# Seven products for the first head groups of pairs 2 and 3, and a new order around them

## The chip, the core and the metric

The kernel runs on one core of one Trainium2 chip. TensorE (PE, with its weight loads PEld) multiplies, VectorE (DVE) and ScalarE (ACT) work on tiles, GpSimd (POOL) and SyncE (SP) mostly issue transfers. The metric is device time in microseconds of one launch; shorter is better.

## What is computed

Two layers on a sequence of 512 tokens of width 1024, each with a SwiGLU feed-forward (width 2816) behind it, and a last RMS norm. The first layer's mixer is attention over three groups of eight heads of width 128: each group has its own query, key and value columns and its own window and dilation, and a softmax over the groups' log-sums joins them. The second layer's mixer is an mLSTM of eight heads.

```python
def dilated_attention_mixer(xn, positions, w_in, w_out):
    proj = (xn @ w_in).reshape(B, S, N_GROUPS, 3, ATTN_HEADS, ATTN_HEAD_DIM)
    for g, (window, dilation) in enumerate(DIL_CONFIGS):
        q = apply_partial_rope(proj[:, :, g, 0], positions) * scale
        k = apply_partial_rope(proj[:, :, g, 1], positions)
        o, lse = dilated_window_attention(q, k, proj[:, :, g, 2], window, dilation)
        ...
    wts = jax.nn.softmax(jnp.stack(lses), axis=0)
    o = jnp.einsum('gbsh,gbshd->bshd', wts.astype(xn.dtype), jnp.stack(outs))
    return o.reshape(B, S, ATTN_WIDTH) @ w_out

def reference(...):
    for i in range(DEPTH):
        h = h + (attention if i % 2 == 0 else mlstm)(rms_norm(h, ...))
        h = h + swiglu(rms_norm(h, ffn_norm[i]), ffn_w_in[i], ffn_w_out[i])
    return rms_norm(h, final_norm)
```

## The kernel before, in words

Every large matrix is multiplied in float32 as three products of a high and a low part: `split_chunk` (L216) makes a weight chunk's high part by a copy on ACT (L223) and its low part by a difference on DVE (L225), and PE runs high x high, high x low and low x high.

**The work in attention.** The eight heads go in four pairs (`project_pair`, L1003), each with groups 0, 1 and 2. A group's queries and keys for a pair are one 1024 x 512 projection. *Plain* (`project`, L260) it is 96 matmuls of 512 columns in four chunks of weights; its results leave by copies (L1033). *By seven products* (`qk_unit`, L902, a Strassen-like scheme) the weights are four quarters W11, W12, W21, W22; the names P1 to P7 are the products, in the order `QK_ORDER` (L861), each of 24 matmuls of 256 columns. `prepare_part` (L880) makes the weights of one product: up to one difference of quarters (L885), then the split, then the loads of the next group's quarters. `finish` (L913) takes sums out of PSUM by ACT copies and two DVE sums (L937). `by_products` (L865) says which groups go so: groups 1 and 2 of every pair.

**After the projections**, per pair (`attention_pair`, L658): `rope` (L603) turns the first 32 rows of queries and keys, packed four quarters to a tile, by four DVE instructions, and ACT or POOL copies them back (L628). `scores0` (L694) multiplies queries by keys for group 0 and takes masked maxima on DVE (L709); `scores12` (L726) does so for groups 1 and 2 (L734, L737), group by group. `exponentials` (L744) run on ACT. `joint` (L779) exchanges maxima and sums between the groups through one small matmul (`xps`, L770) and makes weights; `weigh(i)` (L797) scales head i's exponentials by them on DVE (L802, L805); `transposes(i)` (L807, L811) and `bring(i)` (L817) turn them through DRAM into `pT`; `values(i)` (L822) multiplies them by the values, 30 small matmuls a head.

**What sets the order.** Each engine takes its instructions in one order that the program writes, with edges added by hand: `tc.issue_after(ins)` puts what is traced inside it behind `ins` on its engine; `behind_scores` and `behind_factors` do so for splits on DVE and ACT. A counter of ticks runs along the projections: `advance` (L143) adds one, four times in a plain or seven-product group, and `defer(n, fn)` (L140) puts work n ticks on. So `SCORES0_AT` (L36) is the tick after group 0 at which its scores come, and `RUN_AT` (L37) has, counted from the start of the next pair, the tick of `scores12`, those of joint, weigh, transposes and bring, those of the two heads' values, and those of the loads of the value tiles. `LAST_AT` is the same for the last pair, whose projections are followed by four chunks of value projection (`a3g12v`) and the output projection (`awo`). A `Feed` (L280) holds weight chunks that are split ahead of their product.

**Later parts.** In the mLSTM, `HEAD_AT` (L40) gives each head three ticks, for `decay` (L2112: one matmul, a mask on DVE, ten exponentials on ACT), `scores` (L2128) and `numerators` (L2139). What is due at one tick runs in the order in which it was deferred (L2196). At the end of the kernel, `ends` (L2367) handles the last two blocks of 128 output rows: add, squares (L2300), root and one Newton step (`newton`, L2353), scale, store.

Of the kernel before, what the change touches and what calls it, by code (L numbers as in the profile page):

```python
# [73 lines left out]
def tile_hybrid_dilated_attn_mlstm(  # L74
# [139 lines left out]
    splits = itertools.count()  # L214

    def split_chunk(chunk):  # L216
# [7 lines left out]
        with behind_scores():  # L224
            nc.vector.tensor_tensor(lo[:, :n], raw[:, :n], hi[:, :n].bitcast(F32), op=ALU.subtract)  # L225
        return view(hi), view(lo)
# [177 lines left out]
    with ExitStack() as actx:  # L404
# [9 lines left out]
        mask_band, mask_causal, mask_dil, perm = part(K_MA, 2 * P), part(K_M1, P), part(K_M2, P), part(K_G, P)  # L414
        cosn = ap.tile([P, SEQ], F32, name="cosn")
# [242 lines left out]
        def attention_pair(pr, qks):  # L658
# [35 lines left out]
            def scores0(q, k):  # L694

                for i in range(2):
                    for b2 in range(2):
# [9 lines left out]
                        for b, o, w in parts:  # L707
                            pb = max(2 * b - 1, 0)
                            nc.vector.tensor_tensor_reduce(  # L709
                                p0[i][:, pb:pb + w // P, :].rearrange("p a b -> p (a b)"),  # L710
                                sp[:, o:o + w], mask_band[:, 2 * P - w:], 1.0, -3e38,
                                op0=ALU.add, op1=ALU.max, accum_out=own[:, 0, 0, i, b:b + 1])
                ahead_of_splits[0] = last_on(DVE)
# [4 lines left out]
                if pr < HEADS // 2 - 1:  # L718
                    exps()
                    ahead_of_splits[0], ahead_of_casts[0] = last_on(DVE), last_on(ACT)  # L720
                else:
                    defer(2, lambda: behind(exps, engine=ACT))
# [3 lines left out]
            def scores12(gs=(1, 2)):  # L726

                for g in gs:
# [6 lines left out]
                for g, i in [e for e in ((1, 0), (2, 0), (1, 1), (2, 1)) if e[0] in gs]:  # L735
# [5 lines left out]
                    if g == 2:  # L741
                        exponentials(1, i)

            def exponentials(o, i):  # L744

                if o:
                    nc.vector.tensor_tensor(own[:, 0, 1, i], mx[:, 0, i], mx[:, 1, i], op=ALU.max)
                nc.vector.tensor_scalar(nb[:, o, i], own[:, 0, o, i], -QK_SCALE, None, op0=ALU.mult)
                if o == 0:
# [47 lines left out]
            def weigh(i):  # L797
                cf4 = weight[0]
                for b in range(4):
                    pb = max(2 * b - 1, 0)  # L800
                    blk = p0[i][:, pb:2 * b + 1, :].rearrange("p a b -> p (a b)")
                    nc.vector.tensor_scalar(blk, blk, cf4[:, 0, i, b:b + 1], None, op0=ALU.mult)  # L802
                for c in range(4):
                    blk = p12[i].rearrange("p (g c) k -> p c g k", g=2)[:, c]
                    nc.vector.tensor_scalar(blk, blk, cf4[:, 1, i, c:c + 1], None, op0=ALU.mult)  # L805
# [59 lines left out]
        def by_products(pr, g):  # L865
            return g > 0

        def load_part(pr, g, key):
            if g > 2:
                return  # L870
# [7 lines left out]
            parts_of.setdefault((pr, g), {})[key] = t  # L878

        def prepare_part(pr, g, name):  # L880
# [10 lines left out]
            elif name == "P7":  # L891
                less("W12", "W22", "W12")
            whl = split_chunk((b[src], 1024, four_k, "a%dg%d%s" % (pr, g, name)))
            if name == "P7":
                less("W21", "W21", "W11")
                for key in ("W11", "W12"):
                    load_part(pr, g + 1, key)
            elif name in ("P3", "P4"):
                load_part(pr, g + 1, src)
            return whl  # L900

        def qk_unit(pr, g, qk):  # L902
# [9 lines left out]

            def finish(name):  # L913
                nonlocal rot, vu
                if name == "P5":
                    vu = ap.tile([P, 2, SEQ], F32, tag="vu", name=nm + "vu")
                    nc.scalar.activation(vu[:, 0], acc["p5"], AF.Copy)
# [4 lines left out]
                elif name in ("P2", "P4"):  # L922
                    th = int(name == "P4")
                    src = two_m(acc[target[name]])
                    if th == 0:
                        t = ap.tile([P, 2, SEQ], F32, tag="rot", name="rot")
                        rot = t[:, 0], t[:, 1]
                    pack(th, src[:R])
                    nc.scalar.activation(halves(qk[0], th), src, AF.Copy)
                    ahead_of_casts[0] = last_on(ACT)  # L930
                    if last and th:
                        rope(qk, rot, False, 1, 2, True)
                elif name in ("P7", "P3"):
                    th = int(name == "P7")
                    out = halves(qk[1], th)
                    with behind_scores():
                        nc.vector.tensor_tensor(out, two_m(acc[target[name]]), two_m(vu[:, 1 - th]), op=ALU.add)  # L937
                    if g == 2:
                        ahead_of_splits[0] = last_on(DVE)
                    pack(2 + th, out[:R])  # L940
                    if g == 2:
                        ahead_of_casts[0] = last_on(ACT)
                    if last and th == 0:
                        rope(qk, rot, False, 0, 1, True)
                        rope(qk, rot, False, 2, 4, True)

            for n, name in enumerate(QK_ORDER):
# [3 lines left out]
                if name == "P5":  # L951
                    acc["u"] = acc_tile(nm + "u")
                    nc.scalar.activation(acc["u"], acc["c11"], AF.Copy)
                    ahead_of_casts[0] = last_on(ACT)
# [32 lines left out]
                if n == 6 and last:  # L987
                    ahead_of_splits[0] = last_on(DVE)
                if n == 6 and not last:
                    back = rope(qk, rot, False)  # L990
                    if g == 2:
                        back()
                        ahead_of_splits[0], ahead_of_casts[0] = last_on(DVE), last_on(ACT)
                    else:
                        defer(1, lambda: behind(back, engine=ACT))
                if n in (1, 3, 5, 6):
                    advance()
                if n:
                    feed.fill(feed.ahead + 1)
            if pr:  # L1000
                feed.ahead = 3

        def project_pair(pr, qks, then=None):  # L1003
            nm = "a%d" % pr
            for g in range(3):
# [5 lines left out]
                if by_products(pr, g):  # L1011
                    qk.extend(tok_tile("%sg%d_%s" % (nm, g, "qk"[part])) for part in range(2))
                    qk_unit(pr, g, qk)
# [915 lines left out]
    with ExitStack() as mctx:  # L1929
# [302 lines left out]
    with ExitStack() as fctx:  # L2232
# [134 lines left out]
        def ends(acc, tb, cs):  # L2367
# [17 lines left out]
            tb2, scaled = held.pop()  # L2385
            r2 = fr[:, tb2:tb2 + 1]
# [3 lines left out]
            rows2 = slice(tb2 * P, (tb2 + 1) * P)  # L2390
# [3 lines left out]
            nc.sync.dma_start(out[rows2, 0:512], scaled)  # L2394
            r = after(DVE_, lambda: newton(tb))
            after(ACT_, lambda: nc.scalar.activation(ht[tb, 1], ht[tb, 1], AF.Copy, scale=r))
            nc.scalar.dma_start(out[rows, 512:1024], ht[tb, 1])
            for c in (slice(0, 256), slice(256, 512)):
                nc.vector.scalar_tensor_tensor(t0[:, c], t0[:, c], r, gbc[0][:, c], op0=ALU.mult, op1=ALU.mult)
                nc.sync.dma_start(out[rows, c], t0[:, c])  # L2400
# [54 lines left out]
```

## Time and profile before

| | |
|---|---|
| median of 3 runs (lowest to highest) | 1384.47 us (1384.03 to 1384.59) |
| the profiled execution's own time | 1384.39 us |
| its span | 1382.6 us, 22873 instructions |
| granted TensorE clock over the span | 0.998 |
| HBM read, written | 167.30 MB, 22.54 MB |

The profile is of one execution. Times inside it count from the start of its span. A tile is named by the program: `a2g1P_h` is the high part of a weight chunk of pair 2, group 1; `a2s` are scores, `a2p` exponentials, `a2o` outputs of pair 2; `_l` is a low part. A row of a view may end in the idle time of the engine just before and, after `<-`, what ended it. Matmuls overlap, so their rates are read from the distance between starts and not from the length of one.

### The profile page before, as it was taken

The page shows a single profiled execution, that of the slowest core. Times are in us where ns is not written, and L with a number is a line of the kernel's source. Part 1 is how long each engine was busy: PE and PEld are TensorE (multiplying, and loading weights), DVE is VectorE, ACT ScalarE, POOL GpSimd, SP SyncE. Part 2 cuts the span into 40 slices and gives each one's busy share as a digit, 9 for nine tenths or more (in the row PEclk, how much of TensorE's full clock was granted, in tenths as well). Part 3 has the DMA queues.
Part 4 walks back from the last instruction along what each step waited for, and adds up shares of the span by engine and source line. Part 5 has one row for each costly group of instructions (what it writes and reads, how often), then busy time and mean ns, then how long its engine had stood idle before and what let it go on. Part 6 is the DMA issues. An engine that isn't in the chain of part 4 may idle for free. (4 is left out here: it accounts for less than half of the span.)

```text
span 1382.6 us, 22873 instructions
## 1 busy us (share of the span) xinstructions
PE 1366.5 (99%) x8884; PEld 1248.1 (90%) x8884; DVE 1124.5 (81%) x1856; ACT 789.4 (57%) x1254; POOL 182.8 (13%) x266
## 2 busy tenths in 40 slices
PE   9999999999999999999999999999999999999997
PEld 7898889899998889999999998888888999999886
DVE  7988679696896589788778798898758988887887
ACT  6766565666554354444476464795535454448854
POOL 3000013131211010000010110132102330001113
PEclk9999999999999999999999999999999999999999
DMA  9354246547386256323362743324335653335863
GB/s 308 114 176 142 90 136 193 165 141 218 107 275 206 93 137 182 123 66 118 123 161 69 168 125 91 93 66 120 93 119 127 162 166 104 123 123 132 189 167 99
DMA packets 140004, 193.82 MB, mean 140 GB/s; under 512 B 8980, under 2 KB 104788, under 8 KB 139896
## 3 DMA queue, kind: packets, MB, share of 16 engines
q1 hardware_dynamic: 119840, 140.33, 32.4%
q0 software_dynamic: 18832, 51.70, 15.9%
q8 instruction: 70, 1.15, 0.3%
q10 hardware_dynamic: 1224, 0.34, 0.1%
q14 instruction: 38, 0.31, 0.1%
HBM read 167.30 MB, written 22.54 MB: 137 GB/s over the span
## 5 line engine op out<-in xcount | busy, mean ns | idle before, releaser
L1713 POOL DMA_DIRECT2D f1T<-in_ffn_w_out_dram x15 | 18.0, 1199 | 208.2 <-DMA f1P_2w_w<-in_ffn_w_out_dram 135.5
L1688 POOL DMA_DIRECT2D f0S<-in_ffn_w_out_dram x10 | 8.8, 898 | 259.2 <-DMA f0S<-in_ffn_w_out_dram 191.0
L2245 POOL DMA_DIRECT2D hD<-hB x32 | 21.8, 698 | 68.3 <-DVE hB L2242 68.3
L255 PE MATMUL mo<-n_h,mo_k_l 128*128 128x512 f32 x64 | 25.3, 396 | 0.0
L255 PE MATMUL mo<-n_l,mo_k_h 128*128 128x512 f32 x64 | 25.2, 394 | 0.0
L255 PE MATMUL mo<-n_h,mo_k_h 128*128 128x512 f32 x64 | 25.2, 393 | 0.0
L255 PE MATMUL awo<-ao_h,awo_k_h 128*128 128x512 f32 x64 | 25.2, 393 | 0.0
L255 PE MATMUL mqk<-n_h,mqk_k_h 128*128 128x512 f32 x64 | 25.1, 393 | 0.0
L255 PE MATMUL mwo<-yo_l,mwo_k_h 128*128 128x512 f32 x64 | 25.1, 393 | 0.0
L255 PE MATMUL mqk<-n_l,mqk_k_h 128*128 128x512 f32 x64 | 25.1, 392 | 0.0
L255 PE MATMUL f0j<-n_h,f0j_h 128*128 128x512 f32 x64 | 25.0, 391 | 0.0
L255 PE MATMUL f1j<-n_h,f1j_h 128*128 128x512 f32 x64 | 25.0, 391 | 0.0
L255 PE MATMUL awo<-ao_h,awo_k_l 128*128 128x512 f32 x64 | 25.0, 391 | 0.0
L255 PE MATMUL mwo<-yo_h,mwo_k_l 128*128 128x512 f32 x64 | 25.0, 391 | 0.0
L255 PE MATMUL mqk<-n_h,mqk_k_l 128*128 128x512 f32 x64 | 25.0, 390 | 0.0
L255 PE MATMUL awo<-ao_l,awo_k_h 128*128 128x512 f32 x64 | 25.0, 390 | 0.0
L255 PE MATMUL f1j<-n_h,f1j_l 128*128 128x512 f32 x64 | 24.9, 390 | 0.0
L255 PE MATMUL f0j<-n_h,f0j_l 128*128 128x512 f32 x64 | 24.9, 390 | 0.0
L255 PE MATMUL f0j<-n_l,f0j_h 128*128 128x512 f32 x64 | 24.9, 389 | 0.0
L255 PE MATMUL f1j<-n_l,f1j_h 128*128 128x512 f32 x64 | 24.9, 389 | 0.0
L255 PE MATMUL mwo<-yo_h,mwo_k_h 128*128 128x512 f32 x64 | 24.9, 391 | 0.0
L225 DVE TENSOR_TENSOR v1P_l<-v1W,v1P_h 128x1024 fp32r<-128x1024 f32 x14 | 17.1, 1224 | 9.2 <-ACT v1P_h L223 9.1
(2673 smaller groups left out, 5943.5 us busy)
## 6 DMA issues: line engine op xcount, KB each, us to landing
f0j_w<-in_ffn_w_in_dram SPq DMA_DIRECT2D x17, 512.0 KB, 5.3
f1j_w<-in_ffn_w_in_dram SPq DMA_DIRECT2D x17, 512.0 KB, 5.8
f1T<-in_ffn_w_out_dram POOLq DMA_DIRECT2D x15, 512.0 KB, 7.4
f0hid<-in_ffn_w_in_dram SPq DMA_DIRECT2D x9, 512.0 KB, 5.3
f1hid<-in_ffn_w_in_dram SPq DMA_DIRECT2D x9, 512.0 KB, 5.0
v0W<-in_attn_w_in_dram SPq DMA_DIRECT2D x8, 512.0 KB, 8.6
v1W<-in_attn_w_in_dram SPq DMA_DIRECT2D x8, 512.0 KB, 4.7
awo_k_w<-in_attn_w_out_dram SPq DMA_DIRECT2D x8, 512.0 KB, 5.5
```

The source lines that it names most:

```text
L225: nc.vector.tensor_tensor(lo[:, :n], raw[:, :n], hi[:, :n].bitcast(F32), op=ALU.subtract)
L255: nc.tensor.matmul(acc, whl[a][:, k, m * P:(m + 1) * P], pairs[b][kk], start=(kk == 0 and (a, b) == SPLITS[0]), stop=(kk == nk - 1 and (a, ...
L1688: nc.gpsimd.dma_start(t, src[1][:, ks], accum_op=ALU.add)
L1713: nc.gpsimd.dma_start(view(to), weight_rows(hk * UNITS + u, n), accum_op=ALU.add)
L2245: nc.gpsimd.dma_start(hD[k // 4].rearrange("(b i) x -> i b x", i=R)[:, :, c0:c0 + R], t[R * a_:R * (a_ + 1)])
```

## The change

Eight edits.

1. Group 0 of pairs 2 and 3 goes by seven products (`PRODUCTS_FROM`). Its results are written in block order (`each`), its rotated rows packed and copied back by POOL, as in the plain group 0. The weights of the next pair's group 0 are loaded during group 2.
2. In `prepare_part` the difference that P4 needs, and the load of the next W11, move from P7 to P2.
3. `scores0` comes a tick later (7), so between P3 and P4 of group 2. Ahead of it the next pair's first weight chunks are prepared, and the low parts of those that are prepared there (`late`) run on DVE behind the first head's maxima. Negated maxima and exponentials follow head by head; the second head's exponentials are held to the group's end.
4. `scores12` takes both groups at once, block by block: 8 maxima of 256 columns in place of 16 of 128 and of a maximum between the groups.
5. The second head's exponentials are weighed by ACT, but for the last pair.
6. The values of a pair move from ticks 11 and 12 to 14.4 and 15.4, into group 0 two pairs on; the loads of value tiles move from ticks 2, 3, 1 to 4, 5, 4. In the last pair, group 2's scores move from tick 1 to 2, the joint step from 2 to 3, the loads of values from 1 to 4, and the last two of six stored heads are fetched four ticks later. The last pair's rotation is no longer done in three parts.
7. In the mLSTM all decays are deferred first, then all scores, then all numerators: at one tick they run in that order.
8. In the last output step the third block's two halves are scaled on DVE and ACT, and stored by SP, as soon as their Newton step is done, and not on POOL and ACT after the last block's sums; the last block is scaled and stored in four pieces of 256 columns, on DVE and ACT in turn, three on SP's queue and one on ACT's.

```diff
-SCORES0_AT = 6
-RUN_AT = (1, (4, 4.5, 5, 7, 8, 8, 9), (11, 12), (2, 3, 1))
-LAST_AT = (1, (2,), (), (1, 1, 1))
+SCORES0_AT = 7
+RUN_AT = (1, (4, 4.5, 5, 7, 7, 8, 9), (14.4, 15.4), (4, 5, 4))
+PRODUCTS_FROM = 2
+LAST_AT = (2, (3,), (), (4, 4, 4))
...
+    def run_late(_):
+        while lows:
+            with tc.issue_after(last_on(mybir.EngineType.DVE)):
+                lows.pop(0)()
...
+        def low():
             nc.vector.tensor_tensor(lo[:, :n], raw[:, :n], hi[:, :n].bitcast(F32), op=ALU.subtract)
+        if late[0]:
+            lows.append(low)
+        else:
+            with behind_scores():
+                low()
...
-            for ks in (slice(0, 4), slice(4, 6)):
+            def bring_some(ks):
                 nc.sync.dma_start(t[:, ks], oD[ks].rearrange("k p s -> p k s"))
+            bring_some(slice(0, 4))
+            defer(4, lambda: bring_some(slice(4, 6)))
...
+                    if inner:
+                        behind(negate, 0, i, engine=DVE)
+                        if i and pr:
+                            held_exps.append(lambda i=i: exponentials(0, i, False))
+                        else:
+                            exponentials(0, i, False)
+                        run_late(i)
...
+            def both_groups():
+                for c2 in range(2):
+                    for i in range(2):
+                        sp = banks_[c2, i] = score_bank(i, "%ss12" % nm)
+                        for c in (2 * c2, 2 * c2 + 1):
+                            for g in (1, 2):
+                                q, k = qks[g]
+                                sl, o = slice(c * P, (c + 1) * P), (c % 2 * 2 + g - 1) * P
+                                nc.tensor.matmul(sp[:, o:o + P], q[:, i, sl], k[:, i, sl], start=True, stop=True)
...
+                ahead_of_splits[0] = last_on(DVE)
+                for i in range(2):
+                    exponentials(1, i)
...
+                def times(blk, f):
+                    if i and pr < HEADS // 2 - 1:
+                        nc.scalar.activation(blk, blk, AF.Copy, scale=f)
+                    else:
+                        nc.vector.tensor_scalar(blk, blk, f, None, op0=ALU.mult)
...
-            return g > 0
+            return g > 0 or pr >= PRODUCTS_FROM
...
-            if name == "P7":
+            if name == "P2":
                 less("W21", "W21", "W11")
-                for key in ("W11", "W12"):
-                    load_part(pr, g + 1, key)
+                if follows:
+                    load_part(pr, g + 1, "W11")
+            elif name == "P7" and follows:
+                load_part(pr, g + 1, "W12")
...
-                if n == 6 and not last:
-                    back = rope(qk, rot, False)
-                    if g == 2:
+                if n == 6:
+                    with behind_scores() if g == 2 else nullcontext():
+                        back = rope(qk, rot, g == 0)
+                    if g == 0:
+                        defer(1, lambda: back(True))
+                    elif g == 2:
+                        ahead_of_splits[0] = last_on(DVE)
                         back()
...
+                if g == 2 and n == 5:
+                    late[0] = last or by_products(pr + 1, 0)
+                    feed.fill(feed.ahead + 1)
+                    late[0] = False
...
+            while held_exps:
+                behind(held_exps.pop(0), engine=ACT)
+                ahead_of_casts[0] = last_on(ACT)
...
-        for hh, ts in enumerate(HEAD_AT):
-            for t, fn in zip(ts, (decay, scores, numerators)):
-                at_tick(t, lambda hh=hh, fn=fn: fn(hh))
+        for n, fn in enumerate((decay, scores, numerators)):
+            for hh, ts in enumerate(HEAD_AT):
+                at_tick(ts[n], lambda hh=hh, fn=fn: fn(hh))
...
-                after(DVE_, lambda: newton(TB - 2))
+                r2 = after(DVE_, lambda: newton(TB - 2))
+                tb2, scaled = held.pop()
+                rows2, t1 = slice(tb2 * P, (tb2 + 1) * P), ht[tb2, 1]
+                after(DVE_, lambda: nc.vector.tensor_scalar(scaled, scaled, r2, None, op0=ALU.mult))
+                nc.sync.dma_start(out[rows2, 0:512], scaled)
+                after(ACT_, lambda: nc.scalar.activation(t1, t1, AF.Copy, scale=r2))
+                nc.sync.dma_start(out[rows2, 512:1024], t1)
                 return
...
-            nc.gpsimd.tensor_scalar(ht[tb2, 1], ht[tb2, 1], r2, None, op0=ALU.mult)
-            nc.gpsimd.dma_start(out[rows2, 512:1024], ht[tb2, 1])
-            after(ACT_, lambda: nc.scalar.activation(scaled, scaled, AF.Copy, scale=r2))
-            nc.sync.dma_start(out[rows2, 0:512], scaled)
             r = after(DVE_, lambda: newton(tb))
-            after(ACT_, lambda: nc.scalar.activation(ht[tb, 1], ht[tb, 1], AF.Copy, scale=r))
-            nc.scalar.dma_start(out[rows, 512:1024], ht[tb, 1])
-            for c in (slice(0, 256), slice(256, 512)):
-                nc.vector.scalar_tensor_tensor(t0[:, c], t0[:, c], r, gbc[0][:, c], op0=ALU.mult, op1=ALU.mult)
-                nc.sync.dma_start(out[rows, c], t0[:, c])
+            for n, queue in enumerate((nc.sync, nc.scalar)):
+                c, c1 = slice(256 * n, 256 * (n + 1)), slice(512 + 256 * n, 768 + 256 * n)
+                t, t1 = t0[:, c], ht[tb, 1][:, c]
+                after(DVE_, lambda: nc.vector.scalar_tensor_tensor(t, t, r, gbc[0][:, c], op0=ALU.mult, op1=ALU.mult))
+                nc.sync.dma_start(out[rows, c], t)
+                after(ACT_, lambda: nc.scalar.activation(t1, t1, AF.Copy, scale=r))
+                queue.dma_start(out[rows, c1], t1)
```

More of the change, by code (lines that the diff above doesn't have):

```diff
@@ L891, in prepare_part, with qk_unit @@
             elif name == "P7":
[L892 removed]
+                with tc.issue_after(sixth[0]) if (pr, g) == (1, 2) else nullcontext():
+                    less("W12", "W22", "W12")
             whl = split_chunk((b[src], 1024, four_k, "a%dg%d%s" % (pr, g, name)))
[L894 removed]
+            if name == "P5" and not late[0]:
+                sixth[0] = last_on(DVE)
+            follows = g < 2 or by_products(pr + 1, 0)
+            if name == "P2":
                 less("W21", "W21", "W11")
[L896 to L898 removed]
+                if follows:
+                    load_part(pr, g + 1, "W11")
+            elif name == "P7" and follows:
+                load_part(pr, g + 1, "W12")
+            elif name in ("P3", "P4") and follows:
                 load_part(pr, g + 1, src)
             return whl
[L902 removed]
+        def qk_unit(pr, g, qk, then=None):
             nm = "a%dg%d" % (pr, g)
@@ L911, in pack, with each @@
                 nc.scalar.activation(two_m(rot[0][quarter(q)]), src, AF.Copy)
+            def each(out, src, th, fn):
+                if g:
+                    fn(halves(out, th), *(two_m(t) for t in src))
+                    return
+                for m in range(2):
+                    at = slice(m * HALF, (m + 1) * HALF)
+                    fn(in_order(out[:, m])[:, :, 2 * th:2 * th + 2],
+                       *(t[:, at].rearrange("p (c b j) -> p b c j", c=2, b=TB) for t in src))
             def finish(name):
```

82 lines of the change are left out of this document (50 added, 32 removed).

## The prediction

> **What bounds it.** I read the page first, then the busy time by stage, then the waits. The page:
>
> ```profile
> PE 1366.5 (99%) x8884; PEld 1248.1 (90%) x8884; DVE 1124.5 (81%) x1856; ACT 789.4 (57%) x1254; POOL 182.8 (13%) x266
> ```
>
> TensorE (PE) is busy 99% of the span, so time is won by giving it less work or by closing the few holes. Next the busy time of each engine in stages of the three groups of a pair of attention heads, which the change rewrites. Columns: stage, length, then busy us (instructions) of PE, PEld, DVE, ACT, POOL, the granted clock, the DMA share and GB/s.
>
> ```profile
> core 0: us, PE busy (x) PEld busy (x) DVE busy (x) ACT busy (x) POOL busy (x), PEclk, DMA share, GB/s
> 252.65:278.50 25.85, 25.85 (x134) 21.92 (x133) 17.21 (x59) 14.87 (x33) 3.18 (x5) 1.00 0.48 139
> 278.50:298.58 20.08, 20.08 (x170) 20.08 (x168) 19.98 (x35) 11.17 (x15) 7.87 (x12) 1.00 0.47 149
> 298.58:329.12 30.54, 30.21 (x247) 29.50 (x245) 23.22 (x43) 19.99 (x39) 5.00 (x9) 1.00 0.67 203
> 375.49:406.45 30.96, 30.29 (x247) 29.57 (x245) 28.42 (x53) 16.37 (x24) 5.00 (x9) 1.00 0.81 270
> 432.27:466.00 33.73, 33.73 (x180) 28.89 (x179) 11.30 (x16) 5.93 (x7) 2.19 (x4) 1.00 0.60 188
> ```
>
> The rows 252.65, 278.50 and 298.58 are groups 0, 1 and 2 of pair 2. In group 1, by seven products, PE and PEld both run without a break and DVE is full (19.98 of 20.08). In group 0, plain, DVE has 8.6 us to spare. The matmul rates are in the chain of work that ended last (start, us, what). With 512 columns:
>
> ```profile
> 999.22 40.15 PE mwo L255 x176
> ```
>
> That is 40.15/176 = 0.228 us a matmul. With 256 columns, 2.88/24 = 0.120:
>
> ```profile
> 1105.20 2.88 PE f1j_c L1566 x24
> ```
>
>
> **Group 0 by products.** Plain, a group is 96 matmuls of 512 columns: 96 x 0.228 = 21.9. By seven products it is 168 of 256: 168 x 0.120 = 20.2. The stages say a little more. Group 0's stage also holds the scores of the pair before:
>
> ```profile
> 334.68 3.74 PE L734 MATMUL a2s<-a2g_k,a2g_q 128*128 128x128 f32 x32
> 338.17 0.48 PE L255 MATMUL a3g0q<-xa_h,a3g0q_k_h 128*128 128x512 f32 x1
> ```
>
> They hold PE for 338.17 - 334.68 = 3.49, so the plain group takes 25.85 - 3.49 = 22.4, of which some 0.2 are two small exchange matmuls; group 1 took 20.08. I take 2.1 a group, **-4.2** for pairs 2 and 3 (bounds -3.5 by the rates, -4.6 by the stages).
>
> What it asks of DVE, by the groups of pair 2's stage (busy us, mean ns):
>
> ```profile
> L225 DVE TENSOR_TENSOR a2g2P_l<-a2g2W,a2g2P_h 128x1024 fp32r<-128x1024 f32 x7 | 8.4, 1210 | 0.0
> L885 DVE TENSOR_TENSOR a2g2W<-a2g2W,a2g2W 128x1024 f32<-128x1024 f32 x4 | 4.8, 1209 | 0.0
> L737 DVE CUSTOM_DVE_ANT_0 a1p<-a1s,acst 128x128 f32<-128x128 f32 x16 | 3.6, 282 | 0.0
> L709 DVE CUSTOM_DVE_ANT_0 a2p<-a2s,acst 128x256 f32<-128x256 f32 x6 | 2.3, 421 | 0.2 <-PE a2s L703 0.2
> L802 DVE TENSOR_SCALAR a1p<-a1p,a1cf 128x256 f32<-128x256 f32 (+1 forms) x8 | 2.4, 344 | 0.0
> L805 DVE TENSOR_SCALAR a1p<-a1p,a1cf 128x256 f32<-128x256 f32 x8 | 2.3, 342 | 0.0
> L1033 DVE COPY a2g_k<-a2g0k 128x512 f32<-128x512 f32 x2 | 1.4, 682 | 0.0
> L758 ACT ACTIVATE a1p<-a1p,a1nb 128x256 f32<-128x256 f32 x8 | 4.0, 496 | 3.9 <-DVE a1nb L748 3.9
> ```
>
> Added per pair: 7 splits in place of 4 and 4 differences of weights, 7 x 1.21 = 8.5; 4 sums of 256 columns, not shown before, between the 0.28 of 128 and the 0.68 of 512 columns; 0.42 as for the 256-column row, 1.7. Removed: 4 copies, 2.7; 16 maxima of 128 columns become 8 of 256 (16 x 0.28 - 8 x 0.42 = 1.1); the weighing of the second head goes to ACT, half of 2.4 + 2.3. Net +4.0 on DVE, whose 60.4 of 76.5 us (17.21 + 19.98 + 23.22) become 64.4 of some 74: under the bound, but tight. ACT takes eight scalings at the 0.50 of an exponential and some 6 us of splits and copies on its 46 of 76: it has room. PE alone would hide all of this if DVE's work lay evenly. It doesn't, so I add **+1.0** for new stalls (0 to +4, one DVE difference or split late per group).
>
> **Order.** The values of a pair leave group 2 for group 0 two pairs on, beside the new weight work. That evens out DVE: group 0 becomes 20 + 3.5 + 6.5 = 30 us of PE for about 22 of DVE. The longest stalls of before lie in group 2 (us in total, times, longest):
>
> ```profile
> PE a3g2p L965 <- ACT a3g_q L929: 0.6, 1, 0.6
> PE a1g2u L965 <- DVE a1g2P_l L225: 0.4, 1, 0.4
> ```
>
> They stand behind a full DVE that also weighs the second head there. With that on ACT and the last pair's rotation in one piece I take both, **-1.0** (0 to -1.0, since new work could fill the same holes).
>
> The scores of groups 1 and 2 lose cover. Before, between the end of pair 2's last product and these scores stood one head's values and half of the next projection:
>
> ```profile
> 319.64 1.72 PE L829 MATMUL a1o<-a1pT,a1v 128*128 128x128 f32 x14
> ...
> 322.90 0.36 PE L965 MATMUL a2g2u<-xa_h,a2g2P_h 128*128 128x256 f32 x1
> ```
>
> After it the last quarter is packed, turned and copied back on ACT, from the first to the second of these rows:
>
> ```profile
> 326.05 0.59 ACT L911 ACTIVATE rot<-a2g2u 32x512 f32<-32x512 f32 x1 [1.32 <-PE a2g2u L965]
> ...
> 330.85 1.29 ACT L628 ACTIVATE a2g_k<-rot 32x512 f32<-32x512 f32 x2
> ```
>
> One head's values hold PE 322.90 - 319.64 = 3.26, two heads 6.5. From 326.05 to 332.14 that is 6.1 us, begun 0.2 after PE's last product. Afterwards only two products (5.76) cover this, and both groups' scores start together, so PE waits some 0.5: **+1.0** for the two together, pairs 1 and 2 (0 to +5, two DVE splits per pair in the way). Behind that wait on PE stand the next product and everything else; nothing can pass.
>
> At nothing I cost four moves. The split of the next group 0 that is held back behind the first head's maxima (1.2 on DVE) has the second head's scores and a product of 2.88 as cover; without them it costs its 1.2. The scores of group 0 come one product later, and their exponentials by head, with the values two groups on as cover. The load of W11 moves from P7 to P2 and so ahead of W12 on SP; its buffer is its own. POOL's loads of values wait for the later values and hold up only transfers that are a group ahead; each late one would cost its 3.3.
>
> **End of attention.** The exchange of the last pair moves behind a third value chunk, and a head's values of pair 2 follow it.
>
> ```profile
> 421.38 0.29 DVE L772 TENSOR_TENSOR a3ex<-a3xps,cst 128x128 f32<-128x128 f32 x1 [0.26 <-PE a3xps L770]
> ```
>
> Its weights come back transposed through DRAM, by SP, land so long after the issue, and are first used at the start in the third row:
>
> ```profile
> 440.66 1.96 SPq L819 DMA_DIRECT2D a3pT<-a3pD  x1
> ```
> ```profile
> DMA to landing us min/median/max: 10.0/10.0/10.0
> ```
> ```profile
> L829 PE MATMUL a3o<-a3pT,a3v x28: 271/275/275, 451.4 to 459.0; 128*128 128x128 f32 x28
> ```
>
> Before, two chunks (48 x 0.228 = 10.9) and 84 output matmuls (19.2) lay between exchange and first use of a3pT; now one chunk, 3.3 of values and the 84: 2.2 less. The transfer landed at 440.66 + 10.0 = 450.7; first use was at PE's 451.4, 0.7 spare. SP issued it behind weight loads, which move with PE, so part of the 2.2 is free. SP is also given a late load of heads 4 and 5 (0.5 MB, 2.8 us at the last stage's 188 GB/s), and POOL the last pair's first values. I take **+0.7** (0 to 2.2 - 0.7 + 2.8 = +4.3).
>
> **Decays first.** In the mLSTM, when several pieces are due together, decays now go ahead of numerators.
>
> ```profile
> 933.51 0.37 ACT L2162 ACTIVATE m2j<-m2num,m2rr 128x128 f32<-128x128 f32 x1 [1.34 <-DVE m2rr L2159]
> 933.73 0.69 DVE L2137 SCALAR_TENSOR_TENSOR m4e<-m4s,m4e 128x512 f32<-128x512 f32 x1 [0.25 <-issue]
> ...
> 934.48 0.39 PE L2135 MATMUL m4s<-qs,ks 128*128 128x256 f32 x1 [1.32 <-DVE m4e L2137]
> ```
>
> PE's 1.32 is a wait for a bank that DVE empties after head 2's numerators; ACT idled 1.34 on them with head 4's exponentials queued behind. Ahead of them, most goes: **-1.0** (-1.3 to +1.3, the same wait on a numerator).
>
> **Last outputs.**
>
> ```profile
> 1374.39 0.16 DVE L2357 SCALAR_TENSOR_TENSOR fr<-fa,fr 128x1 f32<-128x1 f32 x1
> 1374.68 0.29 DVE L2298 TENSOR_TENSOR ht<-finlast,ht 128x128 f32<-128x128 f32 x1
> ```
>
> The third block's and then the fourth block's transfers leave after that:
>
> ```profile
> 1376.56 0.33 SPq L2394 DMA_DIRECT2D out_dram<-hlast  x1
> ...
> 1377.17 0.83 SPq L2400 DMA_DIRECT2D out_dram<-ht  x2
> ```
>
> The third block's scaling moves up to 1374.55 on DVE, about 0.5 us (between the 0.42 and 0.68 rows), and holds back the last sum by 0.4; its 0.5 MB leaves 1.4 us earlier and frees the end for four pieces of 128 KB, three of them on SP at 0.41 an issue. **-0.4** (-1.0 to +0.8, three issues in a row and nothing faster).
>
> **Sum:** -4.2 + 1.0 - 1.0 + 1.0 + 0.7 - 1.0 - 0.4 = -3.9. The profiled execution took 1384.39 (its span and 1.8 around it), 0.08 under the median: 1380.5.
>
> **Rivals.** *The gain is eaten:* DVE is full in group 1 and late in group 2, new stalls of 2 us in two pairs: 1380.5 + 4, some 1384. For it speaks 19.98 of 20.08, against it the 2.35 moved to ACT.
>
> *Slower, group 2 loses its cover:* the 6.5 us of values that leave group 2 were what PE did while DVE caught up; group 2 holds 23.2 of DVE work against 20.1 + 2.8 of products and scores left, and DVE itself waits there for products. If half of the 6.5 comes back as stalls in each of pairs 1 to 3, that is 9.8, less the 1.0 already counted: 1389. It turns the sign from (3.9 + 1.0)/3 = 1.6 us a pair on. Against it: the 28.42 of pair 3 falls as its three part-rotations become one, and PE rather than DVE was late before in most of group 2.
>
> *The end waits for a3pT:* +4.3 in place of +0.7, 1384.1.
>
> *Products are no cheaper:* 168 small matmuls lose to 96 large ones if 256 columns cost over 21.9/168 = 0.130 us. Halfway between the two rates, at 0.174, a group would take 29.2, +7.3 instead of -2.1, and the time would be 1399. The 0.120 of row 1105.20 speaks against it. The Trainium skill (TensorE: Matmul & The Clock Gate, Back-to-back issue gap) gives sustained spacings of about 81 ns at 128 columns and 131 at 512; by these, an estimate of 98 at 256, 168 products would take 16.4 against 12.6, and each group would lose 3.8. The trace disagrees with both its spacings (0.120 already at 256 columns, 0.228 at 512) and decides.
>
> **Chances.** Forecast 0.60, eaten 0.15, group 2 without cover 0.14, the end 0.09, products no cheaper 0.02. A measurement of this kernel tells about 0.2% (2.8 us) from no change: the forecast lies beyond it (1377 to 1381.6, its own range), eaten and the end within, the other two mostly above 1387.2. Faster 0.62, same 0.23, slower 0.15. The range 1377 to 1387 leaves out the slower cases and a few hundredths below.
>
> **What would show it.** Group 0 of pairs 2 and 3: 168 matmuls of 256 columns in 20 us of their own; no wait of PE over 0.7 at the scores of groups 1 and 2; group 2's stage near 23 us; a3o without a wait; m4s without its 1.3; last landing 0.4 earlier after PE's end. Wrong if PE waits for splits (L225) or differences (L885) of group 0 or 2 for more than 4 us in all.

## The result and the profile after

| | before | after |
|---|---|---|
| median of 20 runs (lowest to highest) | 1384.57 us (1383.6 to 1387.22) | 1382.37 us (1381.45 to 1383.16) |
| ratio (95% interval) | | 0.9984 (0.9978 to 0.9991) |
| span of the profiled execution | 1382.6 us | 1380.1 us |

The kernel became 2.2 us faster (1.2 to 3.0 by the interval); the forecast was 3.9. PE has less work, as meant, and DVE and ACT have more. The row of the page of the changed kernel that answers to the first one of before:

```profile
PE 1363.8 (99%) x9028; PEld 1253.3 (91%) x9028; DVE 1127.4 (82%) x1782; ACT 806.2 (58%) x1297; POOL 183.0 (13%) x264
```

To find where the 2.5 us between the spans lie, I cut both traces at the same eight matmuls: the first of a1g0q, a2g1c, a3g1c, awo, f0j, mv and mwo, and the last of the kernel. The columns are those of the stage rows in the prediction (stage, length, busy time of each engine, clock, DMA share, GB/s). The kernel before:

```profile
176.45:278.50 102.05, 101.70 (x675) 93.38 (x674) 79.28 (x210) 62.43 (x132) 19.72 (x32) 1.00 0.53 158
278.50:355.03 76.53, 76.20 (x543) 71.49 (x542) 60.52 (x136) 46.13 (x87) 16.04 (x26) 1.00 0.52 162
355.03:432.27 77.24, 76.37 (x543) 71.49 (x542) 67.68 (x156) 45.62 (x86) 16.73 (x28) 1.00 0.63 201
432.27:482.79 50.52, 50.52 (x254) 42.75 (x252) 25.40 (x36) 16.40 (x23) 2.19 (x4) 1.00 0.50 157
482.79:821.35 338.56, 338.44 (x2603) 328.61 (x2602) 284.81 (x339) 184.63 (x238) 17.93 (x18) 1.00 0.47 128
821.35:994.84 173.49, 171.03 (x949) 146.63 (x948) 151.57 (x394) 109.97 (x245) 32.27 (x50) 1.00 0.34 92
994.84:1374.37 379.53, 378.53 (x2396) 344.32 (x2395) 309.23 (x386) 210.71 (x274) 56.35 (x66) 1.00 0.51 136
1374.37:1382.62 8.25, 0.27 (x3) 0.13 (x2) 2.54 (x9) 2.25 (x7) 2.21 (x2) 0.64 0.38 140
```

The changed kernel:

```profile
176.78:277.48 100.70, 99.87 (x746) 95.44 (x745) 81.21 (x165) 69.51 (x146) 18.43 (x31) 1.00 0.47 147
277.48:352.14 74.66, 74.22 (x618) 73.53 (x616) 64.66 (x116) 53.13 (x103) 17.36 (x27) 1.00 0.54 166
352.14:428.82 76.68, 76.21 (x546) 71.55 (x544) 61.38 (x144) 50.51 (x98) 17.64 (x27) 1.00 0.66 213
428.82:480.05 51.23, 50.86 (x254) 42.66 (x253) 25.57 (x38) 16.87 (x24) 3.99 (x8) 1.00 0.50 164
480.05:819.43 339.38, 338.43 (x2603) 328.58 (x2602) 285.36 (x340) 185.14 (x239) 17.84 (x18) 1.00 0.46 128
819.43:994.06 174.63, 171.43 (x950) 146.86 (x948) 153.53 (x394) 107.14 (x243) 31.96 (x50) 1.00 0.34 91
994.06:1372.98 378.92, 378.07 (x2396) 344.46 (x2395) 309.80 (x388) 211.17 (x276) 56.28 (x66) 1.00 0.51 137
1372.98:1380.07 7.09, 0.28 (x3) 0.13 (x2) 2.20 (x9) 2.02 (x6) 0.00 (x0) 0.72 0.41 149
```

Row by row, after less before: -1.35, -1.87 and -0.56 in the attention (rows 1 to 3, -3.8 in all), +0.71 at its end, +0.82 in the first feed-forward, **+1.14 in the mLSTM**, -0.61 in the last projections, **-1.16** behind PE's last matmul, and +0.3 ahead of the attention. The three attention rows gained 3.8 us. A stage that was to gain 1.0 lost 1.1, and the end, worth 0.4 in the forecast, gave 1.2.

Two more views name the causes. First, group 0's own matmuls: the sums over the stretches in which PE ran the queries and keys of group 0 and nothing else, for pairs 2 and 3. Before:

```profile
sum 22.21, PE 22.21 PEld 18.29 DVE 13.57 ACT 13.64 POOL 2.23; mean PE 7.40 PEld 6.10 DVE 4.52 ACT 4.55 POOL 0.74
...
sum 22.28, PE 22.28 PEld 18.29 DVE 13.70 ACT 13.94 POOL 2.54; mean PE 7.43 PEld 6.10 DVE 4.57 ACT 4.65 POOL 0.85
```

After:

```profile
sum 20.38, PE 20.38 PEld 20.36 DVE 16.03 ACT 14.90 POOL 2.34; mean PE 5.09 PEld 5.09 DVE 4.01 ACT 3.73 POOL 0.59
...
sum 20.36, PE 20.36 PEld 20.36 DVE 16.00 ACT 15.89 POOL 2.32; mean PE 5.09 PEld 5.09 DVE 4.00 ACT 3.97 POOL 0.58
```

So the products save 1.83 and 1.92 us. Second, the waits of PE in the changed kernel (in all, times, longest), leaving out those ahead of the attention:

```profile
PE m1num L2239 <- DVE m0yt L2261: 1.2, 1, 1.2
PE m1nb L2207 <- ACT m0e L2217: 1.0, 1, 1.0
PE f0j_u L1658 <- ACT f0j4u L1680: 0.9, 1, 0.9
PE f1j_u L1658 <- ACT f1j4u L1680: 0.8, 1, 0.8
PE a1s L781 <- ACT a1g_k L642: 0.8, 1, 0.8
...
PE a2g1u L1046 <- DVE a2g_k L1016: 0.4, 1, 0.4
PE a3g1u L1046 <- DVE a3g_k L1016: 0.4, 1, 0.4
PE a3o L886 <- DMA a3pT<-a3pD: 0.4, 1, 0.4
```

The first two stand in the mLSTM, where m4s has gone from the list. a1s waits in pair 1 only. The waits of group 2 (a1g2u, a3g2p) have gone, those of group 1 are new. The view counts only the time in which the releaser was awaited; by the distance between starts PE lost 0.98 at a1s, 0.60 at each of a2g1u and a3g1u, and 0.53 at a3o.

### The profile page after: what moved, and what is told of

The parts are those of the page before. It is cut to its first block, busy times and chain, and to the rows that moved or that the text cites. A ratio compares the mean times of both kernels' runs of the same rounds, so it can differ in the third digit from the quotient of the medians.

```text
span 1380.1 us, 23153 instructions
## 1 busy us (share of the span) xinstructions
PE 1363.8 (99%) x9028; PEld 1253.3 (91%) x9028; DVE 1127.4 (82%) x1782; ACT 806.2 (58%) x1297; POOL 183.0 (13%) x264
## 3 DMA queue, kind: packets, MB, share of 16 engines
q0 software_dynamic: 18752, 51.43, 15.4%
q8 instruction: 71, 1.16, 0.4%
```

## The experiments

Each kernel ran 4 to 11 times, in rounds with the kernel before on the same chip. The ratio is to that kernel; 0.0010 is 1.4 us. The changed kernel stands at 0.9984. The rounds were on two chips, so two rows are compared by their ratios, and such a difference is good to about 1.5 us only.

| kernel | median us | ratio (95%) |
|---|---|---|
| heads_old: change without edit 7 | 1380.90 | 0.9978 (0.9969 to 0.9987) |
| heads_mixed: only decays first | 1381.77 | 0.9982 (0.9973 to 0.9990) |
| late_decays: decays first for heads 4 to 7 alone | 1380.27 | 0.9972 (0.9962 to 0.9983) |
| before_newheads: before with edit 7 | 1384.96 | 1.0007 (0.9998 to 1.0016) |
| tail_old: change without edit 8 | 1383.01 | 0.9993 (0.9984 to 1.0002) |
| before_newtail: before with edit 8 | 1383.62 | 0.9997 (0.9988 to 1.0006) |
| group0_plain: change without products in group 0 | 1392.54 | 1.0069 (1.0055 to 1.0082) |
| values_back: values in group 2 again | 1400.91 | 1.0119 (1.0105 to 1.0133) |
| weigh_dve: change without edit 5 | 1387.02 | 1.0023 (1.0014 to 1.0032) |
| trans_later: heads_old, turning a tick later | 1378.99 | 0.9960 (0.9948 to 0.9973) |
| turn_behind_sum: trans_later, turning behind a sum | 1379.33 | 0.9963 (0.9950 to 0.9975) |

### The order in the mLSTM: four runs

heads_old and heads_mixed:

```diff
-        for n, fn in enumerate((decay, scores, numerators)):
-            for hh, ts in enumerate(HEAD_AT):
-                at_tick(ts[n], lambda hh=hh, fn=fn: fn(hh))
+        for hh, ts in enumerate(HEAD_AT):
+            for t, fn in zip(ts, (decay, scores, numerators)):
+                at_tick(t, lambda hh=hh, fn=fn: fn(hh))
```

heads_mixed keeps the loop over decays ahead of this one; late_decays does so for heads 4 to 7 only; before_newheads puts the removed lines into the kernel before.

> The changed kernel with the mLSTM's decays, scores and numerators deferred head by head again, as before the change (edit 7 undone). Theory: putting all scores ahead of all numerators is what costs here. In the changed kernel's stage from 858 to 1000 us PE loses 4.8 us over the nominal distance of its matmuls, before it lost 3.6. Undone, the stage loses 3.6 again, the waits of m1num (1.2) and m1nb (1.0) fall to 0 and 0.4, m4s waits 1.3 again, and the time is 1.2 us below the changed kernel's. Rival: the loss comes from the other state in which the mLSTM is reached (weights that land at another moment, 1.9 us earlier), not from the order: the stage still loses over 4.5 and the time is within 0.4 of the changed kernel's.

> The changed kernel with all decays first but scores and numerators head by head again. Theory: decays first removes the 1.3 wait of m4s, as predicted, and the scores ahead of the numerators make the new wait of m1num; then this order has neither, PE loses about 2.5 to 3.3 us in the stage, and the time is 1.5 to 2.3 us below the changed kernel's. Rival: the decays themselves are the cost (m1nb waits 1.0 for ACT's exponentials of head 0, and the numerators come later because DVE and ACT do masks and exponentials first): the stage loses 4 or more, and the time is within 0.8 of the changed kernel's.

> The changed kernel with decays first for the heads 4 to 7 alone; the heads 0 to 3 go head by head as before. Theory: what edit 7 costs is paid where head 3's decays run ahead of head 1's numerators (ACT waits 3.5 us for m1num, whose buffer they reuse, and m1num waits for m0yt); what it wins is the wait of m4s. Then both come together here: PE loses some 2.2 to 2.8 us in the stage from 858 to 1000 against 4.8 in the changed kernel, no wait of m1num and none of m4s, and the time is 1.7 to 2.4 below the changed kernel's. Rival: the same pattern repeats with the later heads (decays of head 5 ahead of head 3's numerators, and so on), so m3num, m4num or m5num wait instead: the stage loses 3.5 or more, and the time is no better than with the old order.

> The kernel before with edit 7 alone (all decays deferred first, then scores, then numerators). Theory: the order of the mLSTM costs by itself, whatever comes before it: m4s no longer waits 1.3, m1num waits 1.2 and m1nb 1.0, PE loses 4.6 to 5.0 us in the stage instead of 3.6, and the time is 0.9 to 1.3 above the kernel before. Rival: in this kernel, which comes to the mLSTM 1.9 us later and with its weights loaded as before, the order gives what was forecast: 1.0 below.

The times differ by about the width of their intervals, so I read the stage from mv to mwo as well. In the rows of before and after above it is 173.49 and 174.63. heads_old:

```profile
820.41:993.82 173.41, 171.13 (x949) 146.64 (x948) 151.46 (x394) 109.86 (x245) 32.20 (x50) 1.00 0.33 92
```

The kernel before with edit 7 alone:

```profile
820.30:994.88 174.58, 171.40 (x950) 146.82 (x948) 153.53 (x393) 107.12 (x243) 31.95 (x50) 1.00 0.33 92
```

heads_mixed takes 174.61, late_decays 173.33. All thirteen profiles divide in the same way: the stage takes 174.52 to 174.69 us in the seven that have all decays first, and 173.33 to 173.49 in the other six. **Shown:** edit 7 costs 1.1 to 1.2 us in either kernel, so it isn't the moment at which the mLSTM is reached. It isn't the scores ahead of the numerators either: decays first alone cost the same, so my first theory for heads_mixed fell and its rival held. It is the decays of heads 0 to 3: with theirs in the old place (late_decays) the wait of m1num is gone. But late_decays didn't win the wait of m4s, which is still 1.0 (as in heads_old), and its stage is no better than that of heads_old: the second half of that theory fell too. In its trace ACT has the first four exponentials of head 4 done at 930.4, but DVE comes to head 4's first product only behind two splits and head 2's short steps:

```profile
928.62 2.36 DVE L233 TENSOR_TENSOR mo_k_l<-mo_k_w,mo_k_h 128x1024 fp32r<-128x1024 f32 x2
...
931.57 1.14 DVE L2229 SCALAR_TENSOR_TENSOR m4e<-m4s,m4e 128x512 f32<-128x512 f32 x2
```

So there the wait stands behind DVE's order and not behind ACT's; no run changed that order.

What the trace shows in the place of the loss, in the changed kernel (start, us, what; in brackets the idle time before and what ended it):

```profile
904.27 0.17 DVE L2256 TENSOR_SCALAR m0s<-m0s 128x4 f32<-128x4 f32 x1 [2.19 <-ACT m0j L2254]
...
914.20 1.11 DVE L2261 TENSOR_SCALAR m0yt<-m0num,m0rr 128x128 f32<-128x128 f32 x4
...
916.77 0.40 ACT L2214 ACTIVATE m3e<-m3d,bcol 128x128 f32<-128x128 f32 x1 [3.54 <-PE m1num L2239]
```

and in the kernel before:

```profile
908.89 1.12 DVE L2169 TENSOR_SCALAR m0yt<-m0num,m0rr 128x128 f32<-128x128 f32 x4
```

m0yt empties the banks that m1num writes next. Head 0's square root, a chain of thirteen short DVE steps, starts at 904.3 in both kernels, but takes 9.9 us instead of 4.6, since a split (1.22), three differences of queries (0.68 each) and pieces of the convolution (0.47 to 0.68) now stand between its steps. So m0yt is 5.3 us later, m1num waits for it, and head 3's exponentials, whose buffers m1num still reads, wait 3.5 us on ACT for m1num. That the DVE order is the link is read from the trace; no run moved these DVE pieces, or gave the exponentials a third buffer.

### The end: two runs

tail_old puts the last step of before back, before_newtail puts the new one into the kernel before; the diff is edit 8's.

> The changed kernel with the last output step of before (edit 8 undone: the third block's halves scaled on POOL and ACT and stored after the last block's sums; the last block in three pieces). Theory: the new order at the end is worth more than forecast. From the start of PE's last matmul to the end of the span it was 8.2 us before and is 7.1 now; undone, it is 8.2 again, and the time 1.1 us above the changed kernel's. Rival: it is worth the forecast 0.4, and the rest of the 1.1 is how transfers happened to land in one profile: 0.4 above.

> The kernel before with edit 8 alone (the new last output step). Theory: from the start of PE's last matmul to the end of the span 7.1 to 7.3 us instead of 8.2, so 1.0 to 1.2 below the kernel before. Rival: the step's gain needs the rest of the change, 0.4 or less below.

The last stage of tail_old is 8.24 us long again, that of before_newtail 7.25 instead of 8.25. By the ratios tail_old's time is 1.2 above the changed kernel's, and before_newtail's is 0.4 below before, with an interval from -1.7 to +0.8 (its median is 0.4 above that of before in the same rounds, 1383.19). So the times alone don't decide between theory and rival. The profiles do: from the start of PE's last matmul to the end of the span it is 8.2 to 8.3 us in the three that have the old step and 7.1 to 7.4 in the ten that have the new one. Where it comes from, in the changed kernel:

```profile
1373.22 0.33 SPq L2478 DMA_DIRECT2D out_dram<-hlast  x1
1373.29 0.29 DVE L2390 TENSOR_TENSOR ht<-finlast,ht 128x128 f32<-128x128 f32 x1
...
1375.05 0.16 DVE L2449 SCALAR_TENSOR_TENSOR fr<-fa,fr 128x1 f32<-128x1 f32 x1
```

The last sum starts 0.31 after PE's last start (1372.98), as before (1374.68 against 1374.37): the added scaling holds nothing up. The last Newton step ends at the same distance too (2.2). From there to the end of the span it was 6.0 us before (from 1376.62) and is 4.9 now (from 1375.21), with 0.5 MB and not 1 MB still to be stored. That this is the reason is read from the trace; the two halves of edit 8 weren't run apart.

### Pair 1's scores: a transfer, not the lost cover

trans_later, besides heads_old:

```diff
-RUN_AT = (1, (4, 4.5, 5, 7, 7, 8, 9), (14.4, 15.4), (4, 5, 4))
+RUN_AT = (1, (4, 4.5, 6, 7, 7, 8, 9), (14.4, 15.4), (4, 5, 4))
```

> The changed kernel with edit 7 undone, as in the run with the old order of heads, and the turning of the first head's exponentials on DVE (transposes) a tick later. Theory: the 1.0 us that PE waits at pair 1's scores (a1s) is the price of a late transfer: in pair 1 DVE turns a0p for 2.2 us ahead of the difference for P4, the load of the next group 0's W11 waits for that difference, and through its split, DVE's maxima and the rotation reach PE; in pair 2 the difference goes first and there is no wait. With the turning behind the difference in both, the wait of a1s falls from 1.0 to under 0.3, and the time is 0.7 to 1.0 below the run with the old order of heads, so 1.6 to 2.2 below the changed kernel's. Rival: DVE's whole load in the group decides, and the order of two instructions only moves the wait: a1s or the next product still waits 0.7 or more.

In the changed kernel's pair 1 the turning (L868) runs ahead of the difference for P4, and the first load waits for that difference:

```profile
229.89 2.18 DVE L868 STREAM_TRANSPOSE a0pB<-a0p 128x1920 f32<-128x1920 f32 x1
231.99 1.19 DVE L946 TENSOR_TENSOR a1g2W<-a1g2W,a1g2W 128x1024 f32<-128x1024 f32 x1
...
233.24 0.37 SPq L936 DMA_DIRECT2D a2g0W<-in_attn_w_in_dram  x1
...
240.75 1.06 ACT L231 ACTIVATE a2g0P_h<-a2g0W 128x1024 fp32r<-128x1024 f32 x1 [1.82 <-DMA a2g0W<-in_attn_w_in_dram]
```

In trans_later the difference goes first:

```profile
230.52 1.22 DVE L946 TENSOR_TENSOR a1g2W<-a1g2W,a1g2W 128x1024 f32<-128x1024 f32 x1
231.65 2.17 DVE L868 STREAM_TRANSPOSE a0pB<-a0p 128x1920 f32<-128x1920 f32 x1
...
231.76 0.37 SPq L936 DMA_DIRECT2D a2g0W<-in_attn_w_in_dram  x1
...
238.95 1.06 ACT L231 ACTIVATE a2g0P_h<-a2g0W 128x1024 fp32r<-128x1024 f32 x1
```

Load and split come 1.5 and 1.8 us earlier, and with them DVE's maxima and the rotation; the wait of a1s is gone, and the stage from a1g0q to a2g1c takes 99.49 us (101.03 in heads_old). So two products can cover the rotation, and in the changed kernel the wait hung on a late weight. This version beats both kernels: 0.9960, 4.7 us below the kernel before it ran with. That is 2.5 below heads_old by the ratios, where 0.7 to 1.0 was expected; the stage explains 1.5 of it, and the rest is within what such a difference is good to.

turn_behind_sum tried the same on the waits of group 1, with an edge that puts the turning behind the sum of P7 (`seventh`), and the turning another tick later:

```diff
-RUN_AT = (1, (4, 4.5, 6, 7, 7, 8, 9), (14.4, 15.4), (4, 5, 4))
+RUN_AT = (1, (4, 4.5, 7, 7, 7, 8, 9), (14.4, 15.4), (4, 5, 4))
...
+            def turn_first():
+                with tc.issue_after(seventh[0]):
+                    transposes(0)
...
```

> The run with the later turning (old order of heads), with the first head's turning on DVE placed behind the sum of product P7 in group 1 by an edge. Theory: the 0.6 us that PE waits before P4 of group 1 in pairs 2 and 3 is DVE's sum of P7, which stands behind 2.2 us of turning and 1.2 of a split; ahead of them it is ready, both waits go, and the time is 0.8 to 1.2 below the run with the later turning (some 5.5 below the kernel before). Rival: DVE is full in group 1 (20.7 of 20.8 us), so what is turned later makes the first splits of group 2 late: PE waits there instead, 0.6 or more a pair, and nothing is won.

Both waits of group 1 went, and the list of waits shows where they went to (trans_later had none there):

```profile
PE a1s L781 <- ACT a1g_k L642: 0.6, 1, 0.6
PE a2s L781 <- ACT a2g_k L642: 0.6, 1, 0.6
```

The rival held, only that PE waits at the scores and not for the splits. The time is that of trans_later. So the two products cover the rotation only while DVE isn't late.

### What the new order can't do without: three runs

```diff
# weigh_dve
-                    if i and pr < HEADS // 2 - 1:
+                    if False:
# values_back
-RUN_AT = (1, (4, 4.5, 5, 7, 7, 8, 9), (14.4, 15.4), (4, 5, 4))
+RUN_AT = (1, (4, 4.5, 5, 7, 7, 8, 9), (11, 12), (2, 3, 1))
# group0_plain
-PRODUCTS_FROM = 2
+PRODUCTS_FROM = 4
```

> The changed kernel with the second head's exponentials weighed by DVE again in all pairs (edit 5 undone). It puts 2.35 us per pair back on DVE. Theory: DVE is what the new stalls of 0.6 in group 1 (its sums come behind splits, 20.7 of 20.8 us busy) and the waits in group 2 hang on, so PE loses 0.5 to 2 us more per pair: 1.5 to 5 above the changed kernel's. Rival: these 2.35 lie where DVE has room (groups 0 and 2, 24 of 31 us busy): within 0.5.

weigh_dve is 5.4 us above the changed kernel by the ratios, a little over the top of the range. The three attention stages are 1.4, 1.3 and 3.1 longer, and the waits stand where DVE is late:

```profile
PE a3s L761 <- DVE a3own L727: 1.5, 1, 1.5
...
PE a1g2c L1046 <- DVE a1g2P_l L233: 1.0, 1, 1.0
...
PE a3g2u L1046 <- DVE a3g2P_l L233: 0.8, 1, 0.8
```

> The changed kernel with the values of a pair back at ticks 11 and 12, in group 2, and their loads back at ticks 2, 3, 1 (part of edit 6 undone). Theory: the move is worth about what the forecast gave it. Back in group 2 the values cover the rotation again, so the 1.0 wait at pair 1's scores (a1s) goes; but DVE's work bunches again in group 2, whose PE lost 0.6, 0.8 and 1.2 us in pairs 1, 2 and 3 before and loses 0.1, 0.3 and 0.4 now: within 1 us of the changed kernel's, rather above. Rival: group 2 lost its cover, and this is what ate the gain: over 1 us below the changed kernel's.

values_back is 18.7 above the changed kernel, so the rival, by which cover in group 2 would win time back, falls. My own size was far too small, and this is no clean price of the move: POOL stores the first head's output ahead of the second head's load, which leaves at 246.9 instead of 239.5 before, and PE waits 2.3 us for it. In pair 2 the same load leaves at 404.7 instead of 393.2, again behind a store, and this is the longest wait of all:

```profile
246.30 0.57 POOL L655 DMA_DIRECT2D oD<-o_keep  x1 [12.58 <-ACT o_keep L654]
246.91 0.55 POOL L876 DMA_DIRECT2D a0pT<-a0pD  x1
```
```profile
PE a2o L886 <- DMA a2pT<-a2pD: 5.3, 1, 5.3
```

> The changed kernel with group 0 plain in all pairs (edit 1 undone by its constant, all else kept: the order of scores, of values, of maxima). Theory: the products of group 0 are where the gain comes from; a2g0 and a3g0 hold PE for 20.4 and 20.3 us by products and 22.2 and 22.3 plain, so 3.8 us come back, less the two waits of 0.6 for DVE in group 1 that the added splits make: 2.6 to 3.8 us above the changed kernel's, so 0.4 to 1.6 above the kernel before. Rival: what was won in group 0 is lost again where DVE is full, in group 1 and behind the scores, so the plain version is under 1.5 us above the changed kernel's.

group0_plain is 11.7 above, not 2.6 to 3.8. The products' own 3.75 is only a part of it: PE also waits 3.6 us at a1s, 1.4 at a2s, 1.7 at a3s and 2.1 at a3o. (These waits are read in a profile of 1396.55 us, 4.0 above the median of the five executions.) The hand-made order around group 0 is fitted to its products, so taking one edit out of eight measured, above all, how the other seven fit without it. For the edit's own price I keep the stretches of its matmuls. The longest wait also cost more than its length. PE in the hole and behind it (the column ahead of the DMA share is the granted clock):

```profile
252.94:256.85 3.91, 0.28 (x4) 0.09 (x2) 1.81 (x3) 1.92 (x4) 0.00 (x0) 1.00 0.00 0
256.85:258.50 1.65, 1.65 (x9) 1.65 (x10) 0.28 (x1) 1.63 (x3) 0.00 (x0) 0.61 0.00 0
258.50:260.50 2.00, 2.00 (x11) 2.00 (x11) 1.63 (x5) 2.00 (x10) 0.00 (x0) 0.50 0.00 0
```

## Why the prediction was right in direction and short of its size

- **Group 0 by products (-4.2): right, a little less, -3.75.** I took 20.08 from group 1, whose products follow each other. In group 0 scores and values stand between them, and each stretch of products behind them takes 0.05 to 0.09 more than its 2.88 a product. The rate held: two products in a row take 5.76, 0.120 a matmul. The Trainium skill (TensorE: Matmul & The Clock Gate, Back-to-back issue gap) gives spacings of 81 ns at 128 columns and 131 at 512, by which the products would have lost; the trace disagrees, as it did before.
- **New stalls from DVE (+1.0): right, about +0.9.** a2g1u and a3g1u lose 0.60 each, where 0 and 0.35 were lost before. They stand in group 1, where DVE is full, now behind turning and a split.
- **Stalls of before that go (-1.0): mis-sized, about -2.** By starts, 0.8 of a3g2p, 0.5 of a1g2u, 0.5 of a2g2p and smaller ones of 0.2 or less went. weigh_dve shows that the weighing on ACT pays for this. But these holes aren't steady: the stage of pair 3 took 77.24, 76.14 and 77.73 us in the three profiles that have the attention of before.
- **The scores without cover (+1.0): the reason wrong, the size right by luck.** 0.98 in pair 1 and none in pair 2, where the forecast had both; it was a late transfer, as trans_later shows. Group 2 took 23.18 to 23.36 us, as forecast.
- **End of attention (+0.7): right, +0.71**, of it 0.53 at a3o for the transfer of a3pT.
- **Decays first (-1.0): the step that failed, +1.14.** I followed the one wait that I saw (m4s behind head 2's numerators) and took it that decays ahead of numerators only fill ACT's idle time. My upper bound named "the same wait on a numerator" and I gave it no chance of its own. The wait of m4s did go in the changed kernel; 1.4 came back at m1num and 0.5 at m1nb. Nor was its cause the one I named: with head 4's decays ahead (late_decays) it is still 1.0, behind DVE.
- **Last outputs (-0.4): mis-sized, -1.16.** I charged the sum with the added scaling (nothing) and three issues in a row, and counted too little for half the bytes at the end: against PE's last start the third block's first half left 2.0 us earlier, not 1.4.
- **Unchanged code: +0.5, not in the sum.** The first feed-forward is 0.8 longer: the transfer f0T1l lands 8.3 us after its issue, not 7.5, a DVE difference waits 3.0 for it instead of 2.2, and f0j_u 0.9 instead of under 0.3. All product versions show this stage at 182.5 to 183.1 from f0j_c to fo, against 181.6 to 181.9 with group 0 plain; why this transfer is slower stays open. A wait of finu for a split (0.7 in the profile of before) comes and goes between profiles of either kind.

These parts come to about -2.7, and the spans differ by 2.5; the rest lies in gaps too small to place. The time, 1382.37, lies above the forecast's own bounds (1377 to 1381.6). Of the rivals, *the gain is eaten* came nearest: some two fifths of it were, but above all in the mLSTM, not in pairs 2 and 3. *Group 2 loses its cover* didn't happen, the end waited 0.5 and not 4.3, and the products were cheaper. Two of the forecast's signs failed: a1s waited 0.98 by starts (none over 0.7 was expected), and a3o waited. Part of the total came out by errors that cancel: the mLSTM's 2.1 in the wrong direction were mostly made up by the holes that went (1.0 more than forecast) and the end (0.8 more).

## What to carry to other kernels

A wait that an order removes must be followed to the buffers that the moved work takes: ask who still reads them, and what then runs later on the engine that frees the next bank. Where one engine is nearly full, look for the late load behind a wait before blaming the engine: swapping two DVE instructions gave 1.5 us here. Undoing one edit of a hand-made order measures how well the rest fits without it; price the edit by its own instructions.

## What the runs showed of the hardware

In group0_plain, after a hole of PE of 3.9 us (rows above), the granted clock was 0.61 and then 0.50 over the next 3.7 us, and matmuls of 128 columns stood 0.21 us apart instead of 0.11, about 1.6 us more. A hole of 5.6 us in values_back, with 0.82 in it, was followed by 0.50 for 3.9 us and 0.76 for 2.0. The Trainium skill (TensorE: Matmul & The Clock Gate, Part 1: The HAM clock gate) says that PE falls to half rate after an idle window of about 3.4 us and needs as long of work to return, and the first agrees; the second took longer to return. But in group0_plain a hole of 2.2 us at a3o was followed by 0.74 and 0.50 as well (over 3.9 us), which that rule doesn't give, while holes of 1.7 to 2.5 us elsewhere left it at 1.00. Why stays open.
